# Dealing the plain weight pieces otherwise among the pairs of a decoder block

## The chip, the cores and the metric

The kernel runs on one core of a Trainium2 chip. The metric is the device time of one launch in microseconds (us), the median over runs. The kernel before takes 1506.3 us (three runs, 1502.62 to 1506.42).

## What is computed

One decoder block on 256 tokens of width 2048, in float32. A mixer runs a gated linear attention (GLA) beside a short gated convolution, merges the two, and projects; a SwiGLU follows, and a last norm.

```python
proj = rmsnorm(x) @ w_in          # q, k, v, g, gk_low, gate_b, gate_c, xc, merge_a, merge_b
o    = rmsnorm(gla_chunked(q, k, v, log_g)) * silu(g)                 # y_a
y_b  = gate_b * causal_depthwise_conv(gate_c * xc, conv_w)
h    = x + (sigmoid(merge_a) * y_a + sigmoid(merge_b) * y_b) @ w_out
h    = h + (silu(n(h) @ w_gate) * (n(h) @ w_up)) @ w_down             # hidden width 5632
out  = rmsnorm(h)
```

In the kernel's names gc, xc, gb, g, ma, mb are gate_c, xc, gate_b, g, merge_a, merge_b, in blocks of 512 columns (gc0 to gc3 and so on); fg and fu are gate and up of the SwiGLU (blocks 0 to 10); dn is w_down, wo is w_out.

## The kernel before, in words

**Pieces.** All weights come as pieces of 128 partitions by 1024 fp32 (512 KB, two tiles of 128x512), in one list, `stream_list` (L192). For every piece ScalarE (ACT) makes a rounded copy, hi (`high`, L259), and VectorE (DVE) the rest, lo = piece - hi (`low`, L264). TensorE (PE) then makes each product out of three matmuls, hi and lo of the weights with hi and lo of the activations (`mm3`, L368 to L370). `take` (L356) keeps five pieces loaded ahead of the one in use; there are six hi buffers, five lo buffers and five raw buffers.

**Plain pieces.** An ordinary product (`eights`, L396) uses a piece for both halves of the tokens, t = 0 and t = 1: 12 matmuls a piece, 8 pieces a key of 512 columns. Each half accumulates in a PSUM bank of its own, taken from three lent banks (`lent`), and a key's last piece drains half 0 as soon as its matmuls are issued, then half 1 (`done`): for g an ACT Silu (L1024), for gb an ACT copy (L1030), for ma and mb an ACT Sigmoid (L1014) and a DVE product out of the same bank (L1015), for dn a DVE add (L1199). The next key takes the third bank for its half 0, and the old key's first bank for its half 1.

**Pairs of seven.** Two blocks that are needed together (gc with xc, fg with fu, v2 with v3) are computed as a 2x2 block product by Winograd's form with seven products in place of eight (`sevens`, L421). `seven_list` (L102) gives its 28 pieces: four quads of sums, q = 0 to 3, each of `11`, `t1`, `t3`, `t2`, `t4`, and then eight operands that are no sums, `21` and `22` (the "twos"). A piece of these has 6 matmuls. `11`, `21` and `22` are loaded as they are; `t1`, `t3`, `t2`, `t4` are sums of loaded blocks, each one more DVE operation of full width (L280 and L286 in `sum_of`) ahead of its hi and lo. The block `y` of `11` has one buffer and is used up to `t2`; the sums `t3`, `t2`, `t4` are built up in place in one tile `x`, so each has to wait until hi and lo of the sum before it are made. At the end of the last quad the partial results are drained: ACT copies the bank of `11` (L437), and after `t2` three DVE operations of half width follow one another (L446, L448, L449), of which L449 reads the bank of `t1`; `22` accumulates onto that bank. After `t4` comes L453, and after the last `22` L460.

**The order.** The DVE and ACT work of a piece is written about five pieces ahead of its matmuls; the drains are written where the piece that ends them is used, and convolution, merging and transposes are put off by so many pieces (`later`, `at`; the convolution's five products L999 come 7, 10, 13, 16 and 19 pieces after a gates pair ends). The framework's scheduler may exchange neighbours in an engine's queue, except where `pin` holds them.

**Where plain pieces go.** Plain pieces are mixed into the pairs so that PE has work while DVE makes sums. `mixed` (L109) puts so many plain pieces behind each of the 28 pieces (`gaps`). Without a list of gaps it puts one behind each sum of the quads, and if some are left, one behind each of the twos. Each of the four gates pairs has 24 plain pieces (three keys of 8, `GATES`, L74), so one behind every sum and every two. The seven SwiGLU pairs fg3 to fg7, fg9 and fg10 have 16 or 15 (`SEVENS`, L88): one behind every sum (with 15 the last `t4` has none), none behind a two. The pairs (v2, v3) and (fg0, fu0) have orders of their own (`HEADS`, `FIRST`).

Of the kernel before, what the change touches and what calls it, by code (L numbers as in the profile page):

```python
# [19 lines left out]
KC = D // P  # L20
# [23 lines left out]
def plan():  # L44
# [29 lines left out]
GATES = (  # L74
    (("gc0", "xc0"), ("g1", "gb0", "mb0")),
    (("gc1", "xc1"), ("ma1", "gb1", "mb1")),
    (("gc2", "xc2"), ("g2", "ma2", "gb2")),
    (("gc3", "xc3"), ("mb2", "g3", "ma3")),
    (None, ("gb3", "mb3")),
)  # L80
# [5 lines left out]
FIRST = {0: (6, 6, 8, 10, 12), 1: (14, 14, 16, 18, 20), 2: (22, 22, 23, 24, 26), 3: (28, 28, 29, 30, 31)}  # L86
FIRST_END = (31, 32)
SEVENS = ((3, 16), (4, 15), (5, 16), (6, 15), (7, 16), (9, 15), (10, 15))  # L88
PLAIN = (1, 2, (0, (0, 1, 2)), (1, (3, 4, 5)), 8, (2, (6, 7, 8)))


# [10 lines left out]
def seven_list(pair):  # L102

    out = [(what, q) for q in range(4) for what in ("11", "t1", "t3", "t2", "t4")]
    twos = (("21", 0), ("21", 1), ("22", 0), ("21", 2), ("22", 1), ("21", 3), ("22", 2), ("22", 3))
    return [(pair, e) for e in out + list(twos)]


def mixed(pair, eights, gaps=None):  # L109


    if pair is None:
        return eights
    sevens = seven_list(pair)
    sums = ("t1", "t3", "t2", "t4")
    if gaps is None:
        gaps = [0] * len(sevens)
        rest = len(eights)
        while rest > 0:
            for some in (sums, ("21", "22")):  # L120
                for n, (_, e) in enumerate(sevens):
                    if e[0] in some and rest > 0:
                        gaps[n] += 1
                        rest -= 1
    assert sum(gaps) == len(eights)
    out, put = [], 0
    for e, n in zip(sevens, gaps):
        out += [e] + eights[put:put + n]
        put += n
    return out  # L130


def gates_list():
    return [e for pair, keys in GATES
            for e in mixed(pair, [(key, k) for key in keys for k in range(0, KC, 2)])]


def heads_list():


    step = {"k": 4, "q": 4, "v": 2, "g": 2}
    plain = [(key, k) for key in ("k1", "q1", "v1", "k2", "q2", "k3", "q3", "g0") for k in range(0, KC, step[key[0]])]
    n = len(plain) - 1 - sum(HEADS)
    gate = [("ma0", k) for k in range(0, KC, 2)]
    return plain[:n] + mixed(("v2", "v3"), plain[n:-1], HEADS) + gate[:4] + plain[-1:] + gate[4:]
# [6 lines left out]
def down_of(part, n, f):  # L152

    first = 4 * (f - PARTS[part][0])
    return [(f"dn{part}_{n}", k) for k in range(first, first + 4, PIECE // DOWN[part][n][1])]


def hidden_list():

    plain = []  # L160
    for what in PLAIN:
        if isinstance(what, tuple):
            part, fs = what
            plain += [e for n in range(len(DOWN[part])) for f in fs for e in down_of(part, n, f)]
        else:
            plain += [(f"{name}{what}", k) for name in ("fg", "fu") for k in range(0, KC, 2)]
    plain = [(f"wo{n}", k) for n in range(1, 4) for k in range(0, KC, 2)] + plain

    before = {(what, q): FIRST[q][n] for q in range(4) for n, what in enumerate(("11", "t1", "t3", "t2", "t4"))}
    pair = seven_list(("fg0", "fu0"))  # L170
    for n, (_, e) in enumerate(pair[20:]):
        before[e] = FIRST_END[0] + n * (FIRST_END[1] - FIRST_END[0]) // 7
    out, put = [], 0
    for key, e in pair:
        out += plain[put:before[e]] + [(key, e)]
        put = before[e]
    plain = plain[put:]
    for f, n in SEVENS:
        out += mixed((f"fg{f}", f"fu{f}"), plain[:n])
        plain = plain[n:]  # L180
    return out + plain

# [9 lines left out]
def stream_list():  # L192

    pieces = [(p[0], p[3]) for p in piece_list()]
    out = [e for e in pieces if e[0] in ("k0", "q0", "v0")] + heads_list() + gates_list()
    out += [e for e in pieces if e[0] == "wo0"]
    return out + hidden_list() + down_list()
# [3 lines left out]
def block_kernel(ctx, tc, x, xt, cols_in, gkw_in, gku_in, gnw, conv_w, finw, w_in, w_out, w_gu, w_dn, out):  # L201
# [873 lines left out]
    for n in run(order + gates_list(), begin):  # L1075
        if n == order.index(("ma0", 6)):

            gla.close()
            oside = ctx.enter_context(tc.tile_pool(name="oside", bufs=1))
            held["pool"] = ctx.enter_context(tc.tile_pool(name="xy", bufs=1))  # L1080
            ew = mix.enter_context(tc.tile_pool(name="ew", bufs=1))
# [77 lines left out]

    act = {}  # L1160
    order = hidden_list()

    base = count["tick"]
# [183 lines left out]
```

## Time and profile before

| | |
|---|---|
| time, median of 3 runs | 1506.3 us |
| the profiled execution's time, its span | 1505.51 us, 1503.7 us |
| busy: PE, weight loads, DVE, ACT | 1485.7, 1239.4, 1310.4, 873.3 us |
| the gates with their four pairs, in the trace | 245.15 to 668.64 us |
| the seven SwiGLU pairs, in the trace | 865.49 to 1440.80 us |

PE is busy for 99% of the span, DVE for 87%, ACT for 58%. The time of an instruction is from its start to its modelled end; consecutive matmuls overlap, so what a matmul costs is read from start to start. A wait of PE shows as a larger distance between two starts, and in square brackets behind the row where PE was idle, with the instruction that ended the wait. Rows of DVE and ACT with "x2" are two instructions merged, and their time is that of both.

### The profile page before, as it was taken

How to read it: one execution, taken by the hardware profiler on the slowest of the kernel's cores; microseconds unless marked ns; L12 is line 12 of the kernel's file. 1: busy time of each engine (PE TensorE's matmuls, PEld its weight loads, DVE VectorE, ACT ScalarE, POOL GpSimd, SP SyncE). 2: the span in 40 equal slices, each digit the busy share in tenths (PEclk: the TensorE clock that was granted, in tenths of full speed). 3: DMA queues.
4: the chain of work that ended last, by engine and by line, in shares of the span. 5: the costliest groups of instructions: out<-in, count | busy, mean ns of one | idle time of the engine just before them, and what ended most of it. 6: DMA issues, size and time to landing. Idle time of an engine off the chain costs nothing.

```text
span 1503.7 us, 19400 instructions
## 1 busy us (share of the span) xinstructions
PE 1485.7 (99%) x7040; PEld 1239.4 (82%) x7040; DVE 1310.4 (87%) x1314; ACT 873.3 (58%) x993; POOL 33.0 (2%) x59
## 2 busy tenths in 40 slices
PE   9999999999999999999999999999999999999998
PEld 8989988888788788888888888888888788888887
DVE  7898878978988989966789999999998999999975
ACT  7755565654565565554556756655564556565553
POOL 0010000001001001000000000000000000000000
PEclk9999999999999999999999999999999999999999
DMA  9666677787786778787666777876776878787782
GB/s 352 216 184 184 200 231 254 244 264 225 239 294 207 269 263 268 259 274 212 216 218 213 239 249 251 254 260 222 271 239 226 264 253 277 238 268 230 231 299 93
DMA packets 101280, 362.78 MB, mean 241 GB/s; under 512 B 11620, under 2 KB 11748, under 8 KB 101056
## 3 DMA queue, kind: packets, MB, share of 16 engines
q1 hardware_dynamic: 97808, 350.92, 71.4%
q0 software_dynamic: 2800, 8.89, 2.3%
q10 hardware_dynamic: 576, 1.72, 0.3%
q8 instruction: 55, 0.90, 0.2%
q14 instruction: 41, 0.34, 0.1%
HBM read 355.23 MB, written 2.10 MB: 238 GB/s over the span
## 4 chain that ended last, share of the span: by engine, by line
PE 88%; DVE 6%; issue 3%; DMA 2%; ACT 1%; SPq 0%; DVEq 0%; ACTq 0%
PE fg L368 8%; PE fg L370 8%; PE fg L369 8%; PE dn L368 5%; PE dn L370 5%; PE dn L369 5%; PE gc L368 3%; PE gc L370 3%; PE gc L369 3%; DVE lo L264 2%; DMA raw<-in_w_in_dram 2%; PE wo L368 2%; PE gb L368 2%; PE wo L370 2%; PE wo L369 2%
## 5 line engine op out<-in xcount | busy, mean ns | idle before, releaser
L264 DVE TENSOR_TENSOR lo<-raw,hi 128x1024 fp32r<-128x1024 f32 (+1 forms) x502 | 608.5, 1219 | 93.4 <-ACT hi L259 17.9
L259 ACT CAST hi<-raw 128x1024 fp32r<-128x1024 f32 (+1 forms) x502 | 519.8, 1047 | 229.5 <-PE mb L370 30.2
L259 ACT CAST hi<-x 128x1024 fp32r<-128x1024 f32 x156 | 164.2, 1053 | 314.3 <-DVE x L286 239.9
L264 DVE TENSOR_TENSOR lo<-x,hi 128x1024 fp32r<-128x1024 f32 x156 | 190.8, 1223 | 38.7 <-ACT hi L259 27.3
L368 PE MATMUL dn<-lo,acth 128*128 128x512 f32 (+1 forms) x368 | 140.9, 383 | 3.2 <-DVE h L1199 2.4
L286 DVE TENSOR_TENSOR x<-x,raw 128x1024 f32<-128x1024 f32 x104 | 126.8, 1220 | 16.0 <-DMA raw<-in_w_in_dram 10.3
L370 PE MATMUL dn<-hi,acth 128*128 128x512 f32 (+1 forms) x368 | 139.9, 380 | 0.0
L369 PE MATMUL dn<-hi,actl 128*128 128x512 f32 (+1 forms) x368 | 139.9, 380 | 0.0
L368 PE MATMUL fg<-lo,hh 128*128 128x512 f32 x288 | 112.5, 391 | 0.1
L370 PE MATMUL fg<-hi,hh 128*128 128x512 f32 x288 | 112.2, 390 | 0.0
L369 PE MATMUL fg<-hi,hl 128*128 128x512 f32 x288 | 112.2, 389 | 0.0
L368 PE MATMUL fg<-lo,sh 128*128 128x512 f32 x256 | 101.0, 395 | 0.0
L369 PE MATMUL fg<-hi,sl 128*128 128x512 f32 x256 | 99.9, 390 | 0.0
L370 PE MATMUL fg<-hi,sh 128*128 128x512 f32 x256 | 99.8, 390 | 0.0
L368 PEld LDWEIGHTS dn<-lo,acth 128*128 128x128 f32 x368 | 69.2, 188 | 17.7 <-DVE h L1199 3.9
L370 PEld LDWEIGHTS dn<-hi,acth 128*128 128x128 f32 x368 | 69.2, 188 | 13.3
L369 PEld LDWEIGHTS dn<-hi,actl 128*128 128x128 f32 x368 | 69.2, 188 | 12.9
L280 DVE TENSOR_TENSOR raw<-y,x 128x1024 f32<-128x1024 f32 x52 | 63.4, 1219 | 3.3 <-DMA y<-in_w_gu_dram 2.9
L264 DVE TENSOR_TENSOR lo<-y,hi 128x1024 fp32r<-128x1024 f32 x52 | 63.4, 1219 | 3.1 <-PE g L368 1.5
L368 PEld LDWEIGHTS fg<-lo,hh 128*128 128x128 f32 x288 | 54.1, 188 | 12.3 <-DVE lo L264 1.1
L286 DVE TENSOR_TENSOR x<-x,y 128x1024 f32<-128x1024 f32 x52 | 63.4, 1220 | 0.6
L370 PEld LDWEIGHTS fg<-hi,hh 128*128 128x128 f32 x288 | 54.1, 188 | 11.2
(269 smaller groups left out, 3053.9 us busy)
## 6 DMA issues: line engine op xcount, KB each, us to landing
raw<-in_w_in_dram SPq DMA_DIRECT2D x254, 512.0 KB, 4.7
raw<-in_w_gu_dram SPq DMA_DIRECT2D x176, 512.0 KB, 4.5
raw<-in_w_dn_dram SPq DMA_DIRECT2D x88, 512.0 KB, 4.6
y<-in_w_gu_dram SPq DMA_DIRECT2D x32, 512.0 KB, 4.3
x<-in_w_gu_dram SPq DMA_DIRECT2D x32, 512.0 KB, 4.8
raw<-in_w_out_dram SPq DMA_DIRECT2D x32, 512.0 KB, 4.0
y<-in_w_in_dram SPq DMA_DIRECT2D x20, 512.0 KB, 3.7
x<-in_w_in_dram SPq DMA_DIRECT2D x20, 512.0 KB, 6.0
```

What stands on the lines that cost most here:

```text
L259: nc.scalar.copy(hi[:, ks, :], raw[:, ks, :])
L264: nc.vector.tensor_tensor(out=lo[:, ks, :], in0=raw[:, ks, :], in1=hi[:, ks, :].bitcast(F32), op=ALU.subtract)
L280: nc.vector.tensor_tensor(out=raw, in0=y, in1=held["x"], op=ALU.add)
L286: nc.vector.tensor_tensor(out=x, in0=x, in1=other, op=ALU.add)
L368: nc.tensor.matmul(ps, lhsT=sh, rhs=ml, start=first, stop=False, skip_group_check=onto)
L369: nc.tensor.matmul(ps, lhsT=sl, rhs=mh, start=False, stop=False, skip_group_check=onto)
L370: nc.tensor.matmul(ps, lhsT=sh, rhs=mh, start=False, stop=last, skip_group_check=onto)
```

## The change

`mixed` no longer makes its own gaps. A new function, `dealt`, takes the number of plain pieces in each quad; within a quad it places them behind `t1`, `t3`, `t2`, `t4`, `11`, `t3`, `t2`, in this order of preference, and spreads what is left over the eight twos.

| pair | quads 0, 1, 2, 3 and twos before | after |
|---|---|---|
| gates (24 plain pieces) | 4, 4, 4, 4 and 8 | 5, 6, 6, 4 and 3 |
| SwiGLU with 16 | 4, 4, 4, 4 and 0 | 4, 4, 3, 3 and 2 |
| SwiGLU with 15 | 4, 4, 4, 3 and 0 | 4, 4, 3, 2 and 2 |

So a gates quad of six runs `11` p `t1` p `t3` p p `t2` p `t4` p (p a plain piece), and the 8th and 9th plain piece of a gates pair, the last of its first key and the first of its second, stand beside one another. A quad of three has no plain piece behind `t4`, a quad of two none behind `t2` and `t4`. The two plain pieces among the SwiGLU's twos stand behind the fourth two and behind the last. Number and order of the plain pieces and of the pair's pieces are the same as before, each among themselves.

```diff
+GATES_QUADS = {24: (5, 6, 6, 4)}
+SEVENS_QUADS = {15: (4, 4, 3, 2), 16: (4, 4, 3, 3)}
...
+def dealt(pieces, quads):
+
+    out = []
+    for n in quads:
+        places = [0] * 5
+        for i in (1, 2, 3, 4, 0, 2, 3)[:n]:
+            places[i] += 1
+        out += places
+    rest = pieces - sum(quads)
+    return out + [(i + 1) * rest // 8 - i * rest // 8 for i in range(8)]
...
-def mixed(pair, eights, gaps=None):
+def mixed(pair, eights, gaps):
...
-    if gaps is None:
-        gaps = [0] * len(sevens)
-        rest = len(eights)
-        while rest > 0:
-            for some in (sums, ("21", "22")):
-                for n, (_, e) in enumerate(sevens):
-                    if e[0] in some and rest > 0:
-                        gaps[n] += 1
-                        rest -= 1
...
 def gates_list():
+    out = []
+    for pair, keys in GATES:
+        eights = [(key, k) for key in keys for k in range(0, KC, 2)]
+        out += mixed(pair, eights, dealt(len(eights), GATES_QUADS[len(eights)] if pair else ()))
+    return out
...
     for f, n in SEVENS:
-        out += mixed((f"fg{f}", f"fu{f}"), plain[:n])
+        out += mixed((f"fg{f}", f"fu{f}"), plain[:n], dealt(n, SEVENS_QUADS[n]))
```

More of the change, by code (lines that the diff above doesn't have):

```diff
@@ L106, in seven_list @@
     return [(pair, e) for e in out + list(twos)]
-def mixed(pair, eights, gaps=None):
+def dealt(pieces, quads):
[8 more added lines that the diff above has]
+def mixed(pair, eights, gaps):
     if pair is None:
         return eights
-    sevens = seven_list(pair)
-    sums = ("t1", "t3", "t2", "t4")
-    if gaps is None:
-        gaps = [0] * len(sevens)
-        rest = len(eights)
-        while rest > 0:
-            for some in (sums, ("21", "22")):
-                for n, (_, e) in enumerate(sevens):
-                    if e[0] in some and rest > 0:
-                        gaps[n] += 1
-                        rest -= 1
     assert sum(gaps) == len(eights)
     out, put = [], 0
-    for e, n in zip(sevens, gaps):
+    for e, n in zip(seven_list(pair), gaps):
         out += [e] + eights[put:put + n]
@@ L133, in gates_list @@
 def gates_list():
-    return [e for pair, keys in GATES
-            for e in mixed(pair, [(key, k) for key in keys for k in range(0, KC, 2)])]
+    out = []
[3 more added lines that the diff above has]
+    return out
 def heads_list():
```

## The prediction

> **What bounds the kernel now.** I read the page, then the windows by pair of seven (from a pair's first matmul to the next pair's), then who PE waited for, then the timeline of PE, DVE and ACT around those waits.
>
> ```profile
> PE   9999999999999999999999999999999999999998
> PE 88%; DVE 6%; issue 3%; DMA 2%; ACT 1%; SPq 0%; DVEq 0%; ACTq 0%
> ```
>
> PE is busy in every slice and carries 88% of the chain that ended last. So the change, which moves no work off PE, can win only what PE waits. The windows' columns are the length, then busy us of PE, weight loads (PEld), DVE, ACT and POOL. First the four gates pairs, then the SwiGLU's fg3, 4, 5, 6, 7, 9, 10:
>
> ```profile
> 245.15:348.51 103.36, 103.36 (x458) 85.59 (x456) 86.91 (x77) 60.73 (x62) 0.00 (x0) 1.00 0.77 244
> 348.51:456.27 107.76, 105.40 (x465) 86.07 (x464) 94.77 (x89) 58.04 (x62) 5.01 (x9) 1.00 0.76 251
> 456.27:563.60 107.33, 105.19 (x465) 86.08 (x464) 96.07 (x90) 60.21 (x63) 4.96 (x9) 1.00 0.77 252
> 563.60:668.64 105.04, 104.78 (x465) 86.22 (x464) 92.72 (x87) 59.54 (x63) 4.97 (x9) 1.00 0.82 267
> 865.49:949.02 83.53, 83.53 (x377) 69.15 (x376) 77.97 (x74) 50.80 (x54) 0.00 (x0) 1.00 0.77 249
> 949.02:1029.36 80.34, 80.34 (x361) 66.50 (x360) 75.74 (x72) 45.76 (x48) 0.00 (x0) 1.00 0.77 253
> 1029.36:1112.53 83.17, 83.17 (x373) 68.67 (x372) 77.83 (x75) 46.88 (x50) 0.00 (x0) 1.00 0.75 253
> 1112.53:1195.65 83.12, 81.05 (x357) 65.71 (x356) 76.41 (x74) 45.41 (x48) 0.00 (x0) 1.00 0.75 246
> 1195.65:1279.23 83.58, 82.83 (x369) 68.38 (x368) 79.11 (x76) 47.02 (x51) 0.00 (x0) 1.00 0.79 253
> 1279.23:1360.16 80.93, 80.93 (x365) 66.82 (x364) 75.91 (x72) 48.30 (x52) 0.00 (x0) 1.00 0.79 254
> 1360.16:1440.80 80.64, 80.17 (x358) 65.94 (x356) 75.95 (x74) 46.08 (x49) 0.00 (x0) 1.00 0.74 243
> ```
>
> The four gates pairs do the same products. The first takes 103.36 us without idle time, the next three 4.40, 3.97 and 1.68 more. Some of that is work: eight more weight loads each, for transposes. In the first pair PE loads weights for 85.59/103.36 = 82.8% of the time; at that share the other three would take 103.9, 104.0 and 104.1, so that 3.8 + 3.4 + 0.9 = 8.1 us are waits. Idle PE alone gives 2.36 + 2.14 + 0.26 = 4.8, the bare lengths 10.1: the bounds. The same share on the seven SwiGLU pairs leaves 0.0, 0.0, 0.2, 3.8, 1.0, 0.2 and 1.0, together 6.3 us (by idle PE 2.07 + 0.75 + 0.47 = 3.3).
>
> Here a rule of the Trainium skill bears on the sum: "Perfetto Trace Analysis", section "Identifying the Most-Contended Engine", judges PE's headroom by the busy share of weight loads and not by that of matmuls, which are pipelined. By matmul rows the gates would have 4.8 us to win, by weight loads 8.1. The trace agrees with the rule: the matmul rows below last 0.39 us and start 0.23 apart, so each short wait hides under a row's modelled end.
>
> ```profile
> PE gc L368 <- DVE lo L264: 1.6, 3, 0.8
> PE ma L368 <- ACT ya L1024: 1.6, 1, 1.6
> PE gb L368 <- DVE ya L1015: 1.2, 1, 1.2
> PE dn L368 <- DVE h L1199: 2.4, 2, 1.9
> ```
>
> PE waits for a lo that is late, or for a bank whose drain is late. Both come from a DVE that has fallen behind.
>
> **How far DVE is ahead.** I call lead the time from the end of a piece's lo to its first matmul.
>
> ```profile
> 340.98 1.22 DVE L264 TENSOR_TENSOR lo<-y,hi 128x1024 fp32r<-128x1024 f32 x1
> 348.51 0.39 PE L368 MATMUL gc<-lo,xh 128*128 128x512 f32 x1
> 349.87 0.39 PE L368 MATMUL gc<-lo,sh 128*128 128x512 f32 x1
> 352.76 1.22 DVE L264 TENSOR_TENSOR lo<-raw,hi 128x1024 fp32r<-128x1024 f32 x1
> 353.90 1.22 DVE L286 TENSOR_TENSOR x<-x,raw 128x1024 f32<-128x1024 f32 x1
> 385.81 1.22 DVE L264 TENSOR_TENSOR lo<-raw,hi 128x1024 fp32r<-128x1024 f32 x1
> 387.08 0.50 PE L368 MATMUL gb<-lo,xh 128*128 128x512 f32 x1 [0.33 <-DVE lo L264]
> ```
>
> The second gates pair begins with a lead of 348.51 - 342.20 = 6.3 us, and two quads later it is 387.08 - 387.03 = 0.05: PE waits. From the same rows, start to start: a piece of the pair costs PE 349.87 - 348.51 = 1.36 (a plain one, with twice the matmuls, 2.72), and an operation of full width costs DVE 353.90 - 352.76 = 1.14.
>
> **The change part by part.** Nothing is added or removed; the same pieces come in another order, so the direct cost is nothing and all is in the lead. A quad with n plain pieces gives PE 5 x 1.36 + 2.72n = 6.80 + 2.72n, and DVE five lo, four sums and n more lo, 10.26 + 1.14n. PE's surplus, which is time for DVE's other work, is -0.3, 1.3, 2.9, 4.4 and 6.0 us for n = 2 to 6. The eight twos: 1.8 + 1.58n, so 1.8, 4.9, 6.5 and 14.4 for n = 0, 2, 3, 8.
>
> *Gates.* The quads go from 4 x 2.9 = 11.4 to 4.4 + 6.0 + 6.0 + 2.9 = 19.3, the twos from 14.4 to 6.5. The side work that starves DVE in pairs two to four (up to 96.07 - 86.91 = 9.2 us more of DVE than in the first: convolution, gating, merging) falls mostly in quads 0 to 2. At the place of the wait at 387.08 the new order has given DVE 1.6 + 3.2 = 4.8 us more, a lead of about 4.8 where it was 0.05, and quad 2 adds 3.2. I take off all 8.1.
>
> Against this stands the neighbourhood of the 8th and 9th plain piece. The half 1 of the new key needs the bank of the old key's half 0. Before, two pieces of the pair lay between (2.72 us); now none, and PE comes to that bank 0.23 + 1.36 = 1.6 us after the start of the old key's last matmul. When was it drained before?
>
> ```profile
> 280.28 0.39 PE L370 MATMUL g<-hi,xh 128*128 128x512 f32 x1
> 280.40 1.26 ACT L1024 ACTIVATE ya<-g,r 128x512 f32<-128x512 f32 x2
> 389.22 1.28 DVE L1015 TENSOR_TENSOR ya<-ya,ma 128x512 f32<-128x512 f32 x2
> 389.95 0.50 PE L368 MATMUL gb<-lo,xh 128*128 128x512 f32 x1 [1.21 <-DVE ya L1015]
> 598.73 0.39 PE L370 MATMUL mb<-hi,xh 128*128 128x512 f32 x1
> 601.43 0.68 DVE L1015 TENSOR_TENSOR sb<-sb,mb 128x512 f32<-128x512 f32 x1
> ```
>
> g1 (first pair) was free after about 0.8 us, half of the two rows merged: no wait. mb2 (fourth pair) was free 602.11 - 598.73 = 3.4 us after, too late by 1.8. ma1 (second pair), drained from 389.22 on, was so late that PE waited even with two pieces between (389.95), but at a lead near zero. A lead of 5 brings the drains of ma1 and mb2 to perhaps 2.8, a wait of 1.2 each; g2 (third pair), with ACT alone, lies between g1's nothing and that, 0.6. That puts back 3.0, with bounds of 0 (the scheduler lets the next piece of the pair pass) and 3 x 1.8 = 5.4. Gates: -8.1 + 3.0 = -5.1.
>
> *SwiGLU.* Here quads 2 and 3 lose 1.58 each and the twos gain 3.16, so DVE has no more time in all: 75.7 to 79.1 us of busy DVE in windows of 80.3 to 83.6 leave little. What can be won is the time that DVE, far ahead, stood and waited for PE to free a buffer (929.31 below, in fg3), and can now work. I take half of the 6.3 us, -3.1; bounds 0 and -6.3. Against it:
>
> ```profile
> 929.31 1.23 DVE L264 TENSOR_TENSOR lo<-raw,hi 128x1024 fp32r<-128x1024 f32 x1 [1.33 <-PE fg L368]
> 930.64 0.39 PE L370 MATMUL fg<-hi,sh 128*128 128x512 f32 x1
> 934.53 0.69 DVE L449 TENSOR_TENSOR u<-fg,v 128x512 f32<-128x512 f32 x1
> 1163.85 1.22 DVE L264 TENSOR_TENSOR lo<-y,hi 128x1024 fp32r<-128x1024 f32 x1
> 1167.11 0.39 PE L368 MATMUL fg<-lo,hh 128*128 128x512 f32 x1
> 1173.21 1.23 DVE L264 TENSOR_TENSOR lo<-x,hi 128x1024 fp32r<-128x1024 f32 x1 [1.17 <-ACT hi L259]
> 1179.99 0.39 PE L370 MATMUL fg<-hi,sh 128*128 128x512 f32 x1
> 1184.78 0.68 DVE L449 TENSOR_TENSOR u<-fg,v 128x512 f32<-128x512 f32 x1
> ```
>
> 930.64 and 1179.99 are the last matmuls of the last `t2` in fg3 and fg6. L449 ends 4.6 us later in fg3, where the lead was long, and 5.5 in fg6. The first `22` needs it. Before, one plain and three pair pieces lay between, 0.23 + 2.72 + 4.08 = 7.0 us; in the four pairs with 15 the plain one is gone, and PE arrives after 4.3. It would wait 0.3 to 1.2 us; I take 0.75, and 4 x 0.75 = 3.0 (bounds 1.2 and 4.8). The reload of `y`, which has one buffer, comes due 1.14 sooner after a quad of three; it costs only where the lead is short, and by the windows' shares that is fg6, fg7 and fg10: 0 to 3 x 1.14 = 3.4 us, taken as 0, since a lead of over 1.14 hides it. SwiGLU: -3.1 + 3.0 = -0.1.
>
> **Sum:** -5.1 - 0.1 = -5.2 us. The profiled execution took 1505.51, so 1500.3; against the median of 1506.3 that is **1501.1 us**. About 0.3% (4.5 us) is what a measurement of this kernel can tell from no change, so 1501.8 is the line.
>
> **The rivals.**
>
> *Both halves win.* The scheduler passes the pair's next piece over the busy bank, as far as data allow, and the flatter lead empties the SwiGLU's waits: -8.1, and -6.3 + 3.0 = -3.3: 1494.9 with all of it, 1497 in the middle. For it: the waits of fg6 (3.8 of the 6.3) need only a lead some 2 us longer. Against: DVE's total there.
>
> *Given back.* The key switch costs 5.4, and the late L449 what the flatter lead wins or more, +1.5: -8.1 + 5.4 + 1.5, about -1: 1505. For it: mb2's 3.4 us with a lead that was not low. The Trainium skill's "Perfetto Trace Analysis", section "Matmuls", wants independent groups to rotate through banks so that one's evacuation overlaps the next one's matmuls; adjacent keys on three banks shorten just that overlap, and the row at 389.95 is such a wait.
>
> *Slower: the last quad of two.* Its `t2` and `t4` stand together, so DVE waits for ACT between them, as at 1173.21 (1.17 us), and its surplus falls from +1.3 with three to -0.3 - 1.2 = -1.5. It decides if the lead at the quad's start is under about 3 us; in fg6 it was 1167.11 - 1165.07 = 2.0. Then each of the four pairs pays some 1.5 for the lead and 1.2 for L449, nothing of the 6.3 is won, and the gates bring 5.1: -5.1 + 4 x 2.7 = +5.7, 1512.
>
> That the change does nothing is no rival: eleven pairs of seven get another order.
>
> **How the numbers follow.** The forecast 0.42 (1499 to 1503.5, a little over half of it below 1501.8: 0.24 faster, 0.18 same); both win 0.24, all faster; given back 0.22, all within 0.3%; slower 0.12. So faster 0.48, same 0.40, slower 0.12. The range runs from 1495 (the second case whole) to 1507 (given back, and the gentlest third of the slower case).
>
> **What would show it.** Right: the second to fourth gates pairs at 105 us or less, no wait of gc for lo; short waits of gb and g for L1015 in the second and fourth; in fg4, fg6, fg9 and fg10 a gap of about a microsecond ahead of the first `22`, with L449 as its releaser; leads in the middle of the twos higher than before. Wrong: gates pairs still at 107, or the SwiGLU pairs together longer or shorter by over 4 us.

## The result and the profile after

The changed kernel takes 1529.3 us (median of 4 runs, 1527.16 to 1529.92), the kernel before, run beside it, 1505.5 (4 runs, 1502.62 to 1506.42): a ratio of 1.0159 with a 95% interval of 1.0141 to 1.0177. It is 24 us slower, where 5.2 less was forecast. The profiled execution took 1528.92 us, its span 1527.1 (before 1503.7).

From the page of the changed kernel, PE's busy share in 40 slices and the shares of the chain that ended last:

```profile
PE   9999999999899998999999999999999999999997
PE 82%; DVE 7%; DMA 4%; issue 3%; ACT 2%; POOL 1%; DVEq 0%; ACTq 0%; SPq 0%
```

Two slices have fallen to 8, both among the gates (382 to 420 and 573 to 611 us), and PE's share of the chain from 88% to 82%. The windows of the changed kernel by pair of seven, first the four gates pairs, then fg4, fg6, fg9 and fg10, the SwiGLU pairs with 15 (the column ahead of the DMA share is PE's granted clock):

```profile
245.83:349.19 103.36, 103.36 (x457) 85.58 (x456) 87.17 (x78) 60.87 (x62) 0.00 (x0) 1.00 0.73 242
349.19:461.23 112.04, 106.13 (x466) 87.20 (x465) 95.96 (x88) 59.65 (x62) 5.00 (x9) 0.98 0.78 241
461.23:567.36 106.13, 104.80 (x466) 86.25 (x464) 95.07 (x89) 61.07 (x63) 4.95 (x9) 1.00 0.79 251
567.36:681.43 114.07, 107.38 (x465) 88.14 (x464) 95.89 (x89) 60.79 (x63) 4.96 (x9) 0.96 0.79 251
961.88:1043.06 81.18, 80.63 (x361) 66.42 (x360) 75.79 (x73) 46.86 (x50) 0.00 (x0) 1.00 0.73 247
1126.67:1211.66 84.99, 81.43 (x357) 65.65 (x356) 78.05 (x76) 45.22 (x48) 0.00 (x0) 1.00 0.74 241
1295.49:1379.84 84.35, 82.35 (x366) 66.34 (x364) 76.15 (x72) 47.43 (x52) 0.00 (x0) 1.00 0.73 242
1379.84:1462.96 83.12, 80.79 (x353) 65.32 (x352) 74.89 (x72) 45.28 (x48) 0.00 (x0) 1.00 0.71 235
```

The second gates pair is 4.3 us longer than before, the third 1.2 shorter, the fourth 9.0 longer: +12.1. Of the SwiGLU pairs these four are 0.8, 1.9, 3.4 and 2.5 longer, 8.6 of the +9.4 of all seven. The other 1.9 of the 23.4 us by which the span grew lie in the heads and the tail. PE's waits in the changed kernel, longest sums first (us in all, times, longest):

```profile
PE g L374 <- DVE sb L1021: 6.7, 1, 6.7
PE gb L374 <- DVE ya L1021: 5.9, 1, 5.9
PE fg L374 <- DVE lo L270: 4.8, 5, 1.2
PE ma L374 <- ACT ya L1030: 1.3, 1, 1.3
```

Lines stand six higher than before, so L374 is the old L368, L1021 the old L1015. The first, second and fourth row are the three places where two keys now stand side by side, called switches below. They cost more than the wait. This is PE after the second-longest of them, and then the first slow matmul after the longest and the first that starts at full speed again:

```profile
389.26 0.80 PE L374 MATMUL gb<-lo,xh 128*128 128x512 f32 x1 [5.91 <-DVE ya L1021]
389.86 0.63 PE L375 MATMUL gb<-hi,xl 128*128 128x512 f32 x1
390.28 0.63 PE L376 MATMUL gb<-hi,xh 128*128 128x512 f32 x1
...
391.99 0.45 PE L374 MATMUL gc<-lo,sh 128*128 128x512 f32 x1
...
608.40 0.80 PE L374 MATMUL g<-lo,xh 128*128 128x512 f32 x1 [6.69 <-DVE sb L1021]
...
614.04 0.39 PE L375 MATMUL g<-hi,xl 128*128 128x512 f32 x1
```

The starts are 0.42 us apart, not 0.23: PE comes back at half its clock (granted clock 0.50 from 389.26 to 391.99 and 0.51 from 608.40 to 614.04). The six matmuls to 391.99 take 2.73 us, 1.4 more than at 0.227, and the 13 to 614.04 take 5.64, 2.7 more. So 13.9 us of waits and 4.1 of slow clock stand against the 12.1 by which the pairs grew; some 5.9 us were won there all the same. The Trainium skill ("TensorE: Matmul & The Clock Gate", Part 1) says that an idle window of about 3.4 us halves PE's clock until it has been busy about as long; waits of 5.9 and 6.7 us and 2.7 and 5.6 us of slow matmuls agree with that in kind. Its 3.4 us is no lower limit here: in the run with the taps loaded once, below, waits of 2.2 and 2.6 us were followed by slow matmuls too.

Why the drains came so late is seen on DVE, in the changed kernel around the first switch, and in one row of ACT:

```profile
373.01 1.22 DVE L1005 TENSOR_TENSOR u<-u,taps 128x1024 f32<-128x1024 f32 x1
...
375.28 1.22 DVE L292 TENSOR_TENSOR x<-x,y 128x1024 f32<-128x1024 f32 x1
...
381.12 1.22 DVE L270 TENSOR_TENSOR lo<-raw,hi 128x1024 fp32r<-128x1024 f32 x1
386.25 1.23 DVE L286 TENSOR_TENSOR raw<-y,x 128x1024 f32<-128x1024 f32 x1 [3.91 <-DMA y<-in_w_in_dram]
387.39 1.22 DVE L270 TENSOR_TENSOR lo<-x,hi 128x1024 fp32r<-128x1024 f32 x1
388.52 0.68 DVE L1021 TENSOR_TENSOR ya<-ya,ma 128x512 f32<-128x512 f32 x1
```

```profile
383.21 1.23 ACT L1020 ACTIVATE ma<-ma,r 128x512 f32<-128x512 f32 x2
```

Both halves' Sigmoids are through by 384.44, and DVE is idle from 382.34, but the drain L1021 stands in its queue behind the first sum of quad 2, which waits 3.9 us for its `y`, and a lo. The DMA issues of the changed kernel in that stretch, and of the kernel before where it loads the same `y` (KB each, us from issue to landing):

```profile
taps<-in_conv_w_dram POOLq DMA_DIRECT2D x1, 768.0 KB, 10.7
y<-in_w_in_dram SPq DMA_DIRECT2D x1, 512.0 KB, 9.7
```

```profile
taps<-in_conv_w_dram POOLq DMA_DIRECT2D x1, 768.0 KB, 8.8
y<-in_w_in_dram SPq DMA_DIRECT2D x1, 512.0 KB, 3.6
```

Up to `t2` of quad 1, which frees `y` for quad 2 (375.28), nine plain pieces have gone by where it was six. So this sum now stands behind the convolution's third product (373.01), which frees the taps: `y` is issued at 376.53, two microseconds behind the next taps' 768 KB (374.52), and takes 9.7 us. Before, that sum came at 369.44 and the product at 372.99; `y` was issued at 370.68, ahead of the taps (374.50), and took 3.6. What DVE waited for in the second to fourth gates pair, before and after, and then in the seven SwiGLU pairs, before and after:

```profile
DVE lo L264 <- ACT hi L259: 10.2, 25, 1.2
DVE x L286 <- DMA raw<-in_w_in_dram: 4.4, 5, 1.4
```

```profile
DVE raw L286 <- DMA y<-in_w_in_dram: 17.6, 6, 3.9
DVE lo L270 <- ACT hi L265: 6.1, 14, 1.2
```

```profile
DVE lo L264 <- ACT hi L259: 21.5, 30, 1.2
```

```profile
DVE lo L270 <- ACT hi L265: 36.5, 37, 1.3
```

The forecast's sum had neither: 17.6 us of waiting for `y`, of which there was none before, and 15.0 us more of waiting for ACT's hi in the SwiGLU. The second is seen in the last quad of fg9, first before, then after:

```profile
1332.04 1.23 DVE L286 TENSOR_TENSOR x<-x,y 128x1024 f32<-128x1024 f32 x1
1333.18 0.68 DVE L629 TENSOR_TENSOR actl<-trb,acth 128x512 fp32r<-128x512 f32 x1
1333.79 1.22 DVE L264 TENSOR_TENSOR lo<-raw,hi 128x1024 fp32r<-128x1024 f32 x1
1335.06 1.23 DVE L264 TENSOR_TENSOR lo<-x,hi 128x1024 fp32r<-128x1024 f32 x1
1336.32 1.23 DVE L286 TENSOR_TENSOR x<-x,raw 128x1024 f32<-128x1024 f32 x1
```

```profile
1352.31 1.22 DVE L292 TENSOR_TENSOR x<-x,y 128x1024 f32<-128x1024 f32 x1
1354.70 1.23 DVE L270 TENSOR_TENSOR lo<-x,hi 128x1024 fp32r<-128x1024 f32 x1 [1.18 <-ACT hi L265]
1355.96 1.23 DVE L292 TENSOR_TENSOR x<-x,raw 128x1024 f32<-128x1024 f32 x1
1358.36 1.23 DVE L270 TENSOR_TENSOR lo<-x,hi 128x1024 fp32r<-128x1024 f32 x1 [1.17 <-ACT hi L265]
```

Between a sum and its own lo stands ACT's hi of that sum, about 1.2 us in which DVE may do something else. Before, the lo of a plain piece filled it; in the quad of two nothing does. Over the seven pairs DVE's work is the same (538.9 us busy before, 537.3 after), so the 9.4 us by which they grew are idle time of DVE; the wait for ACT's hi rose by more than that, and other waits fell. By the ends of lo and the first matmuls in the trace, fg9 came to its twos with a lead of 7.0 us before and 0.4 after.

### The profile page after: what moved, and what is told of

Its sections match the earlier page's. It is cut to its first block, busy times and chain, and to the rows that moved or that the text cites. A ratio compares the mean times of both kernels' runs of the same rounds, so it can differ in the third digit from the quotient of the medians.

```text
span 1527.1 us, 19377 instructions
## 1 busy us (share of the span) xinstructions
PE 1493.3 (98%) x7040; PEld 1241.3 (81%) x7040; DVE 1310.1 (86%) x1314; ACT 874.6 (57%) x993; POOL 38.9 (3%) x59
## 4 chain that ended last, share of the span: by engine, by line
PE 82%; DVE 7%; DMA 4%; issue 3%; ACT 2%; POOL 1%; DVEq 0%; ACTq 0%; SPq 0%
PE fg L374 6%; PE fg L376 6%; PE fg L375 6%; PE dn L374 4%; PE dn L376 4%; PE dn L375 4%; DVE lo L270 4%; PE gc L375 3%; PE gc L374 3%; PE gc L376 3%; PE wo L374 2%; PE g L374 2%; PE gb L374 2%; PE wo L376 2%; PE wo L375 2%
## 5 line engine op out<-in xcount | busy, mean ns | idle before, releaser
L374 PE MATMUL dn<-lo,acth 128*128 128x512 f32 (+1 forms) x368 | 141.2, 384 | 2.5 <-DVE actl L635 1.4
L292 DVE TENSOR_TENSOR x<-x,raw 128x1024 f32<-128x1024 f32 x104 | 126.9, 1221 | 17.4 <-DMA raw<-in_w_in_dram 12.1
L374 PE MATMUL fg<-lo,hh 128*128 128x512 f32 x288 | 113.9, 396 | 4.8 <-DVE lo L270 4.8
L374 PE MATMUL fg<-lo,sh 128*128 128x512 f32 x256 | 100.6, 393 | 0.5 <-DVE u L455 0.5
L374 PEld LDWEIGHTS dn<-lo,acth 128*128 128x128 f32 x368 | 69.2, 188 | 18.0 <-DVE actl L635 2.2
L286 DVE TENSOR_TENSOR raw<-y,x 128x1024 f32<-128x1024 f32 x52 | 64.3, 1236 | 20.1 <-DMA y<-in_w_in_dram 17.6
L374 PEld LDWEIGHTS fg<-lo,hh 128*128 128x128 f32 x288 | 54.1, 188 | 19.4 <-DVE lo L270 8.8
L265 ACT CAST hi<-y 128x1024 fp32r<-128x1024 f32 x52 | 54.5, 1048 | 16.5 <-DMA y<-in_w_in_dram 6.1
```

What stands on the lines that cost most here:

```text
L265: nc.scalar.copy(hi[:, ks, :], raw[:, ks, :])
L286: nc.vector.tensor_tensor(out=raw, in0=y, in1=held["x"], op=ALU.add)
L292: nc.vector.tensor_tensor(out=x, in0=x, in1=other, op=ALU.add)
L374: nc.tensor.matmul(ps, lhsT=sh, rhs=ml, start=first, stop=False, skip_group_check=onto)
```

## The experiments

Three theories were put up. In the gates: the adjacent keys (H), made bad by a drain that stands in DVE's queue behind a late `y` (D, later Y). In the SwiGLU: the quad of two (Q2, A), or any missing plain piece (B); and, as its cause, that DVE has nothing to fill the time of ACT's hi (W). All times are medians; the gates' and SwiGLU's lengths come from the trace, with 320.1 us for the second to fourth gates pair and 575.3 for the seven SwiGLU pairs before. The first four runs stand beside 1507.2 us for the kernel before, the next four beside 1506.0, then 1506.5 and 1505.2.

**Each half alone.** Gates dealt as changed, SwiGLU as before; then the other way round.

```diff
-SEVENS_QUADS = {15: (4, 4, 3, 2), 16: (4, 4, 3, 3)}
+SEVENS_QUADS = {15: (4, 4, 4, 3), 16: (4, 4, 4, 4)}
```

> The gates' new quads (5, 6, 6, 4) with the SwiGLU dealt as before. Theory H (the loss is at the key switch: the 8th and 9th plain piece are neighbours, and PE waits 6 and 7 us for the drain of ma1 and mb2): the gates' sections keep their +12.1 us (second pair about 112.0, fourth about 114.1 us), the SwiGLU pairs come back to within 1 us of before, time about 1518. Rival Q (the last quad of two in the SwiGLU's pairs with 15 makes the loss, and the gates' waits only move it): about 1506. If both parts act and add: 1529.3 - 9.4 = 1520.

```diff
-GATES_QUADS = {24: (5, 6, 6, 4)}
+GATES_QUADS = {24: (4, 4, 4, 4)}
```

> The SwiGLU's new quads with the gates dealt as before. Theory H: the gates' pairs as before (107.8, 107.3, 105.0 us), and the SwiGLU still has its +9.4 us, nearly all in the four pairs with 15 (fg4, fg6, fg9, fg10): time about 1515. If the SwiGLU's loss came only from a start that the gates had shifted: about 1506. Theory Q alone: 1529.

Measured: 1518.29 us, ratio 1.0081 (1.0063 to 1.0100), and 1516.24, 1.0066 (1.0049 to 1.0083). The two rows below are the second to fourth gates pair of the one, 332.84 us against 320.1, and the SwiGLU pairs of the other, 584.53 against 575.3.

```profile
348.81:681.65 332.84, 318.41 (x1393) 261.71 (x1392) 287.01 (x265) 181.48 (x188) 14.92 (x27) 0.98 0.77 247
```

```profile
867.26:1451.79 584.53, 575.35 (x2549) 469.46 (x2548) 536.71 (x510) 326.61 (x348) 0.00 (x0) 1.00 0.73 246
```

Both halves lose by themselves: 11.1 + 9.0 make 20.1 of about 24 us. So they nearly add; the rest, 3.8 us, is within what the three intervals leave open, and was not followed up.

**Taps loaded once.** The taps of block 0 are loaded and serve all four blocks, so that three of the 768 KB loads are gone; DVE's order stays that of the changed kernel.

```diff
+        if i == 0:
+            held["taps"] = ew.tile([P, 3, 512], F32, tag="taps", name="taps")
+            nc.gpsimd.dma_start(held["taps"], conv_w[:, :, 0:512].to_broadcast([P, 3, 512]))
+        taps = held["taps"]
```

> The kernel after, with the convolution's taps loaded only for the first block and used for all four, so three loads of 768 KB are left out and the outputs of three blocks are those of wrong taps. DVE's order is the same as in the kernel after. Theory D (the drains at the key switch are so late because the load of y, which an addition ahead of the drain in DVE's queue waits for, shares its time with the taps' load: 9.7 and 9.0 us to land): y lands 4 to 5 us after its issue, DVE's wait of 3.9 and 3.2 us ahead of the addition vanishes, PE's waits of 6.1 and 6.9 us fall to about 2.5 each, the granted clock stays at 1.00 behind them, and the second and fourth gates pair take about 106 and 107 us: time about 1516. Rival F (the drain is late by its place in DVE's queue, whatever the loads do): both waits stay within 1 us, time 1529.

Measured: 1521.13 us, 1.0099 (1.0083 to 1.0115); by the ratios 0.6% of the changed kernel's 1.6% is gone. Its waits at the adjacent keys, and what is left of DVE's wait for `y`:

```profile
PE g L374 <- DVE sb L1023: 2.6, 1, 2.6
PE gb L374 <- DVE ya L1023: 2.3, 1, 2.3
PE ma L374 <- ACT ya L1032: 2.2, 1, 2.2
```

```profile
DVE raw L286 <- DMA y<-in_w_in_dram: 8.6, 3, 3.6
```

With no edit but to loads, 6.7 and 5.9 fell to 2.6 and 2.3, and the `y` of quad 2 lands in 4.4 to 4.7 us in place of 8.6 to 9.7: more than half of the late drain is the taps' load's doing, as theory D has it. Two other parts of D's forecast failed. The clock did not stay at 1.00 (over the 5 us behind the waits of 2.6 and 2.2 us it was 0.66; behind that of 2.3 it was 1.00), and the time is 1521 us, not 1516. DVE still waits for `y` three times, once a pair: the `y` of quad 1 is issued while the shifted copies of `u` (L992 to L997 in the changed kernel) are under way, and takes 6.9 to 8.3 us; before the change it was issued ahead of them and took 3.7 to 4.0.

**One pair piece between the keys.** The sixth plain piece of a quad goes behind `11`.

```diff
-        for i in (1, 2, 3, 4, 0, 2, 3)[:n]:
+        for i in (1, 2, 3, 4, 0, 0, 3)[:n]:
```

> The kernel after, with the sixth plain piece of a quad behind 11 and not behind t3, so that one piece of the pair stands between the 8th and the 9th plain piece; everything else is dealt as after. PE comes to the old key's bank 1.36 us later, and in DVE's queue the addition that waits for y no longer stands ahead of the first drain of ma1. Theory A (only the distance counts): PE's waits shrink by 1.4 each, to about 4.7 and 5.5, the clock still falls: time about 1526. Theory D (the addition and its load ahead of the drain count): the wait for ma1 falls to under 2 us and the clock stays up, so about 1520, and with the same for mb2 1512.

Measured: 1521.41 us, 1.0095 (1.0074 to 1.0116). The waits at the switches of the second and the fourth pair fall to 1.9 and 0.7 us, by more than theory A's 1.4 each, and the time is near D's 1520. D's 1512, for both waits gone, was not reached: the SwiGLU half is still in it, and the transposes (tile trb), which use the lent banks too, now wait 4.2 us in all for one to be drained.

**No quad of two, and a quad of two with its pieces elsewhere.** Gates as before in both. First the SwiGLU pairs with 15 get 4, 4, 3, 3 and one; then they keep 4, 4, 3, 2 but the two stand behind `t1` and `t2`, which also gives L455 its old distance to the first `22`.

```diff
-SEVENS_QUADS = {15: (4, 4, 3, 2), 16: (4, 4, 3, 3)}
+SEVENS_QUADS = {15: (4, 4, 3, 3), 16: (4, 4, 3, 3)}
```

> Gates as before; SwiGLU pairs with 15 now 4, 4, 3, 3 and one behind the last two (no quad of two), pairs with 16 as in the changed kernel. In the changed SwiGLU alone the four pairs with 15 took 7.3 us more than before and the three with 16 1.9. Theory A, the quad of two is the cost (its t2 and t4 stand together, its surplus is below zero): the pairs with 15 come back to within 2 us of before in all, the time is 2 to 4 us over before. Theory B, any plain piece taken out of quads 2 and 3 costs, as DVE has no time to give there: the pairs with 15 keep half or more of it, and the time is 5 to 7 us over before.

```diff
-        for i in (1, 2, 3, 4, 0, 2, 3)[:n]:
+        for i in (1, 3) if n == 2 else (1, 2, 3, 4, 0, 2, 3)[:n]:
```

> Gates as before; SwiGLU 4, 4, 3, 2 and two, but the quad of two has its plain pieces behind t1 and t2, so that t2 and t4 no longer stand together and the first 22 comes 7.0 us after t2's last matmul again, as before the change. Theory A1, the arrangement at the end of the quad is the cost (ACT's hi between t2 and t4, and the late L455): the pairs with 15 fall from 7.3 us over before to 2 or less, the time is 2 to 4 us over before. Theory A2, the quad's missing plain piece itself (surplus -0.3 in place of 1.3 us with a lead near zero): the pairs with 15 stay 4 us or more over before, the time 6 to 9 over before.

Measured: 1516.54 us, 1.0069 (1.0051 to 1.0086), with 582.7 us for the SwiGLU pairs, those with 15 still 5.4 over before where it was 7.3; and 1518.80, 1.0082 (1.0067 to 1.0097), with 584.8 us, those with 15 7.6 over. Theory A falls in both forms: a plain piece taken out of quad 2 alone costs most of what the quad of two does (by the medians all of it: 10.5 us over before, against 9.0 for the changed SwiGLU alone), and where in that quad the two pieces stand makes no difference that can be told. B and A2 are nearer, but both times came out above what they gave (10.5 against 5 to 7, 12.8 against 6 to 9), and neither run shows by which way a missing piece costs.

**Keys spaced, with taps as they were and in three parts.** SwiGLU as before; the 24 plain pieces of a gates pair go 5, 6, 5, 5 and 3, two pieces of the pair between any two keys. The second of these runs also loads the taps as three loads of 256 KB, each as soon as its own product is through.

```diff
-GATES_QUADS = {24: (5, 6, 6, 4)}
+GATES_PLACES = [1, 1, 1, 1, 1, 1, 1, 1, 0, 3, 1, 1, 2, 1, 0, 1, 1, 1, 1, 1, 0, 0, 1, 0, 0, 1, 0, 1]
```

> SwiGLU as before the change; gates 5, 6, 5, 5 and 3, placed so that two pieces of the pair stand between the 8th and 9th and between the 16th and 17th plain piece, as before the change. Theory H, the adjacent keys are the whole loss in the gates and the longer lead is a gain: no wait of g or gb over 1.5 us, the second to fourth gates pairs at 106 or less each, the time 2 to 6 us below before. Rival, the quads of five and six cost by themselves (other late drains, transposes that wait for a bank): the three pairs at 107 or more on the mean, the time 1 us below to 5 over before.

```diff
+        taps = [ew.tile([P, 1, 512], F32, tag=f"taps{j}", name="taps") for j in range(3)]
+        for j in (1, 0, 2):
+            nc.gpsimd.dma_start(taps[j], conv_w[:, j:j + 1, i * 512:(i + 1) * 512].to_broadcast([P, 1, 512]))
```

> As the run with spaced keys, and the taps (768 KB in one load) come as three loads of 256 KB into three tiles, each as soon as its own product of the block before is through. Theory D, the taps' load delays the load of y and with it DVE's queue: no load of y between 370 and 390 or 590 and 610 us takes over 7 us, and the second to fourth gates pairs are together 1 to 3 us shorter than with spaced keys alone. Rival, with the keys spaced the late y costs nothing: same within 1 us.

Measured: 1515.40 us, 1.0064 (1.0040 to 1.0089), and 1505.57, 1.0002 (0.9992 to 1.0012). With the keys spaced no wait of g or gb is left, and still the pairs took 330.7 us where H had 318 at most: H alone is not the cause. The first run's DVE waits 23.4 us for `y`, and now gc feels it:

```profile
PE gc L374 <- DVE lo L270: 9.9, 3, 4.0
```

The second loads the same bytes in smaller lots, of which one of 256 KB still stands 0.9 us ahead of `y`: the `y` that took 8.1 to 8.8 us next to the taps takes 5.5 to 6.0, DVE waits 14.6, and 9.8 us of time are back. Theory D's mechanism holds; its price of 1 to 3 us was far too small.

**Taps moved out of the way.** SP's queue loads the next block's taps 4 to 6 us behind the `y` of the last quad (`TAPS_AT` is 32, 34 and 29 in the three runs). This was done with adjacent keys, with spaced keys, and in the kernel before, SwiGLU as before in all. It changes the queue of the load and its time at once.

```diff
+    def load_taps(i):
+        held["taps", i] = ew.tile([P, 3, 512], F32, tag="taps", name="taps")
+        pin(nc.sync.dma_start(held["taps", i], conv_w[:, :, i * 512:(i + 1) * 512].to_broadcast([P, 3, 512])))
...
+        if i < 3:
+            later(TAPS_AT, lambda: load_taps(i + 1))
```

> The changed gates with the adjacent keys, SwiGLU as before, and the taps of the next block loaded from SP's queue a few pieces behind the load of y for the last quad, not as soon as the old taps are through. Theory Y, the new deal puts the load of y for quad 1 behind the taps' load, and DVE's queue stands behind that y: y of quad 1 lands in under 6 us in the second to fourth gates pair, gb and g wait 1 to 2.5 us in place of 5.9 and 6.8, and the three pairs together are 6 to 10 us shorter than with the changed gates alone (332.9): a time about 1508 to 1512. Rival, the adjacent keys make that wait whatever the loads do: gb and g wait over 4 us and the time stays at 1515 or more.

> The spaced keys, SwiGLU as before, taps loaded behind the y of the last quad. Theory Y: the second to fourth gates pairs at 106.5 or less each, the time at or up to 4 us below before (1502 to 1506). Rival, the load of y for quad 0, which in the new deal is issued behind the shifted copies of u and not ahead of them, costs as much as the taps did: gc still waits over 2 us for lo in each pair, time 1509 or more.

> The kernel before with the taps loaded from SP's queue behind the y of the last quad, as in the run with spaced keys (1503.2, ratio 0.9977). If that gain is of the loads alone, this comes out as fast: ratio 0.997 to 0.999. If the gates' deal carries it, with its longer lead, this stays at before within 0.1%: in the kernel before, the y of quad 2 was issued ahead of the taps (370.68 against 374.50) and landed in 3.6 us, so there is nothing to take away but the 3.9 to 4.4 us in which DVE waited for raw and u.

The `y` that the first of these calls quad 1's is quad 2's, the one of the row at 386.25; quad 1's is the one beside the copies of `u`. Measured: 1511.35 us, 1.0034 (1.0024 to 1.0045); 1503.21, 0.9977 (0.9966 to 0.9988); 1501.76, 0.9975 (0.9966 to 0.9984). The second to fourth gates pair of each:

```profile
349.00:680.18 331.18, 319.95 (x1393) 261.85 (x1392) 290.06 (x267) 184.01 (x190) 12.47 (x24) 0.98 0.78 250
```

```profile
348.68:665.19 316.51, 314.94 (x1394) 258.54 (x1392) 287.25 (x266) 181.79 (x190) 12.52 (x24) 1.00 0.80 261
```

```profile
348.73:665.69 316.96, 314.56 (x1394) 258.65 (x1392) 282.81 (x264) 178.13 (x189) 12.53 (x24) 1.00 0.78 259
```

With adjacent keys the `y` of quad 2 lands in 4.4 to 4.9 us and the time of 1511.35 is in Y's range. The profiled execution took 1515.24 us, 3.9 above the median; in it the three pairs are only 1.7 shorter, against the 6 to 10 expected, since waits of 3.5, 3.4 and 2.6 us stand where one key follows another. So neither cause is the whole.

Each run taken against the kernel before beside it, spacing the keys brings 1.7 us with the taps where they were, which is within the intervals, and 8.1 with them moved; moving the taps brings 6.2 with adjacent keys and 12.6 with spaced ones. Taking both away leaves a kernel faster than before, as Y said, though one pair took 106.7 us and not 106.5. But the old deal with the taps moved is as fast: 317.0 us against 316.5, and the ratio is in the range that was given for a gain of the loads alone. The longer lead of a deal with fuller quads brings nothing that can be measured; the load does. Whether its queue or its time does it was not told apart.

**ACT's hi in the SwiGLU.** The sum `t2` goes into a raw buffer of its own, so that DVE can make it while ACT makes hi of `t3`: first in the changed SwiGLU, then in the kernel before.

```diff
+        if what == "t2" and pair[0][:2] == "fg":
+            held["t2"] = wraw.tile([P, 2, 512], F32, tag="raw", name="raw")
+            nc.vector.tensor_tensor(out=held["t2"], in0=x, in1=y, op=ALU.add)
+            return held["t2"]
+        if what == "t4" and pair[0][:2] == "fg":
+            raw = fetch(one, 4 * q + 2)
+            nc.vector.tensor_tensor(out=x, in0=held["t2"], in1=raw, op=ALU.add)
+            return x
```

> The changed SwiGLU deal, gates as before; in the SwiGLU pairs the sum t2 is written into a raw buffer of its own, not in place, so that DVE can make it while ACT makes hi of t3, and t4's sum does not wait for lo of t2. Theory W, a quad of three or two leaves DVE without other work while it waits for ACT's hi of a sum (2.4 us of idle DVE in quad 3 of each pair in the changed kernel): this idle time falls below 1.2 in quad 3, and the seven pairs lose 3 us or less against before in place of 9.2: time 1508 to 1511. Rival, only the missing surplus counts: the loss stays at 6 or more, time 1513 or more.

> The kernel before with that t2 alone. Theory W: the quads of four had little of this idle time (1.2 to 2.4 us a quad where DVE was behind), so the seven pairs win 1 to 4 us, the time 1 to 4 us below before. Rival, the t2 sum takes a raw buffer, so that loads start later: same or up to 4 us above before.

Measured: 1511.46 us, 1.0035 (1.0024 to 1.0045), with 579.0 us for the SwiGLU pairs, 3.7 over before in place of 9.2; the idle time in quad 3 behind ACT's hi is 1.2 us in two pairs and none in five. But the kernel before becomes slower with it: 1520.99, 1.0092 (1.0077 to 1.0107), 585.7 us. That is no clean removal of a wait: the extra raw buffer it takes, or the new order on DVE, makes waits of its own (DVE's for ACT's hi rise from 21.5 to 37.2 us there). The DVE rows show where: added up over the seven pairs, its waits for ACT's hi of the sums in `x` fall from 32.3 to 10.7 us in the changed deal, and those of pieces in raw buffers rise from 5.4 to 21.1; in the kernel before the first stay (18.3 and 18.9) and the second rise from 3.1 to 18.3. So the edit moves the wait to the `t2` in its raw buffer, and only the changed deal has enough of it to lose on the sums. By these two runs alone W is not decided. So W was tried by itself, with the counts of the kernel before: in quad 2 alone the four plain pieces stand behind `11` and `t1`, and none between the sums.

```diff
-        for i in (1, 2, 3, 4, 0, 2, 3)[:n]:
+        for i in (0, 0, 1, 1) if q == 2 and pieces < 24 else (1, 2, 3, 4, 0, 2, 3)[:n]:
```

> Gates and the counts of the SwiGLU as before the change; only in quad 2 of each SwiGLU pair the four plain pieces stand behind 11 and t1, two each, and none between the sums t3, t2, t4. PE's time less DVE's over the quad is the same as before. Theory W (DVE waits for ACT's hi of a sum where no plain piece's lo fills that time): DVE idles 1.5 to 3 us more in quad 2 of each pair, and the seven pairs are 5 to 15 us longer: time 1511 to 1521. Rival, only the count of plain pieces in a quad matters: the seven pairs within 2 us of before, time within 0.2% of before.

Measured: 1527.42 us, 1.0148 (1.0134 to 1.0162). The SwiGLU pairs and what DVE and PE waited for in them:

```profile
868.26:1461.56 593.30, 581.33 (x2553) 468.37 (x2552) 536.99 (x510) 326.28 (x348) 0.00 (x0) 1.00 0.71 241
```

```profile
DVE lo L270 <- ACT hi L265: 40.8, 40, 1.2
```

```profile
PE fg L374 <- DVE lo L270: 10.2, 24, 0.8
```

The same numbers of pieces in every quad, DVE as busy as before (537.0 against 538.9 us), and 18 us lost, more than W's 5 to 15; DVE's wait for ACT's hi rose from 21.5 to 40.8. The edit also makes PE take three sums in a row, but of the 19.9 us by which DVE idles more, 19.3 are this wait. The rival, by which only the count matters, falls. That the changed kernel's 9.4 us come from this wait is read from its trace; whether the count has a share in them was not shown.

## Why the prediction was wrong

**Bound.** That PE carries the time and can only win its waits held; so did the places where it waits. What failed is how DVE's lead was reckoned: as PE's surplus over DVE's busy time, quad by quad. DVE's own waits were left out, and the change moved those. DVE is busy 1310.1 us after as 1310.4 before.

**Gates, -8.1 for the lead.** "A lead of about 4.8" at the end of the first key came out as 3.75, and the waits of gc for lo are gone, as the prediction's signs asked. But the step "I take off all 8.1" failed. With the loads and the keys out of the way a deal with fuller quads (5, 6, 5, 5) has 316.5 us, 3.6 under before, and the old deal with the loads moved has as much. The share of weight loads (the Trainium skill's "Perfetto Trace Analysis", "Identifying the Most-Contended Engine"), which gave 8.1, asked for more than any kernel here reached; the 4.8 of idle PE was nearer.

**Gates, +3.0 for the key switch.** The mechanism was right, for the keys it named, and the size was off: 5.9, 6.7 and 1.3 in place of 1.2, 1.2 and 0.6, and 4.1 us of half clock on top. "A lead of 5 brings the drains ... to perhaps 2.8" took the drain's time from the lead alone. A drain waits for whatever is ahead of it on DVE, and that was a sum whose operand had not landed. Without the taps' loads the same three waits are 2.3, 2.6 and 2.2 us: so even without that load the switch cost about twice to four times its price in the sum, and the load, which the sum left out, made 3.6 and 4.1 us of the two long ones. The reload of `y` was weighed in the SwiGLU alone, and there only as coming due 1.14 us sooner; whether it would meet another load was not asked. The rule to rotate banks (the same page of the Trainium skill, "Matmuls") was on the right side: with two pieces between the keys, waits of g and gb were gone.

**SwiGLU, -3.1 and +3.0.** "DVE has no more time in all" was the step: by counts it has the same, by the trace its waits for ACT's hi grew by 15.0 us. No flatter lead was won. The late L449 (now L455) hardly showed: PE waited for it once, 0.5 us in fg4. The rival of the last quad of two named the wait (1.17 us, as the row after shows) and its price of 2.7 for each of four pairs was near the 8.6 us found, in part by luck, since 1.2 of the 2.7 was for L449; and it gave the wait to the quad of two alone and a chance of 0.12 to a condition that was not needed: fg9 came to quad 3 with a lead of 4.0 us and paid 3.4. Quads of three pay too.

**The sum.** -5.1 became +12.1, and -0.1 became +9.4. The range ended at 1507, with the key switch at its bound of 5.4, the late L449, and a third of the slower case; no term of it held a wait of DVE for a load.

## What to carry to other kernels

When a list of work is dealt otherwise, look at what each in-order engine will stand behind, not at its busy sum: a plain piece between a sum and its own lo was worth up to 1.2 us of DVE each time, though it brought DVE only work. Check for every load with a single buffer which event frees it and which other load is freed near that time; an exchange of the two can move a landing from 3.6 to 9.7 us. And what frees a PSUM bank is only as early as the operation ahead of it in its engine's queue, so two users of few banks want pieces of other work between them.

## What the runs showed of the hardware

- A load suffers beside a large one ahead of it: the 512 KB `y` of quad 2 took 8.6 to 9.7 us when issued 2 us behind a broadcast load of 768 KB, 4.4 to 4.7 at the same place without that load, and 3.6 to 3.7 before the change, ahead of it. Issued 0.9 us behind the 768 KB it took 8.1 to 8.8, behind 256 KB 5.5 to 6.0.
- PE's clock halved after short waits: 2.2 and 2.6 us in the run with the taps loaded once (granted clock 0.66 over the next 5 us), though not after 2.3 in the same run.
- fg6 took from 80.8 to 84.5 us in seven kernels in which its own order was the same. A difference of 2 us in that one pair cannot be put down to an edit; what is said above rests on all pairs together and on the times.
